# Prompt attention scores in three passes on split operands, and HGRN2 levels on running decayed keys and queries

## The chip, the cores and the metric

The kernel runs on one core of a Trainium2 chip. The metric is the device time of one execution in microseconds, taken as the median of several runs. The engines are TensorE (PE, with its weight loads shown as PEld), VectorE (DVE), ScalarE (ACT), GpSimd (POOL) and SyncE (SP), which issues most of the DMAs. Every engine works through its own queue in order and waits for others by semaphores.

## The reference

One layer of a hybrid decoder is computed for a prompt of 512 tokens and a sample group of 8 sequences of 4 tokens (544 columns together, D = 1024). The two parts that the change touches are these:

```python
# dilated attention, 8 heads of 64: three (window, dilation) patterns per query, ALiBi bias,
# the three outputs combined by their softmax denominators
s = jnp.einsum('bqhd,bqjhd->bhqj', q, kg) * (ATT_DH ** -0.5)
s = s - slopes[:, None, None] * dist
...
# HGRN2, 4 heads of 128: S_t = diag(f_t) S_{t-1} + (1 - f_t) outer i_t, o_t = S_t^T q_t, by chunks
f = lb + (1.0 - lb) * jax.nn.sigmoid(hf)
qh = jax.nn.silu(hq) * (HG_DK ** -0.5)
o, s_new = hgrn2_recurrence(qh, 1.0 - f, hi, jnp.log(f), hg_s0)
```

Around them stand the input projection (w_in), w_out, cross attention to a memory of 256 rows, and a gated feed-forward part with a short convolution (D_FF = 2816). All of it is float32.

## The kernel before, in words

All activations lie with the features on the partitions and the 544 tokens along the free axis. A dense product of float32 operands is made of three products of rounded operands (fp32r): each operand is split into a high part and a low rest, and high by high, high by low and low by high are added up in one PSUM bank. Dense banks have the tag "dense" (two of them), side work has "aux" (five) and "dec" (one). Some pairs of column blocks (`MixPair`, and `Pair` in the feed-forward part) are computed by a scheme of seven products in place of eight, whose intermediate sums are kept in SBUF.

Between the dense products PE does the side work: attention of the samples on their cache (`psd`, `psdo`, 32 columns of the array at a time), attention of the prompt (`psS` scores, `psT` transposes, `psO` values) for four pairs of heads, and HGRN2 (`psB`, `psA`, `psL`, `psin`, `psU`, `psu`, `pso`) for four heads.

`prompt_attention(p, q, k, v)` takes a pair of heads. q and k of the two heads lie on rows 0 to 63 and 64 to 127. The scores of query block qb against its 128·qb+128 keys are one float32 product per head, on 64 rows of the array. A float32 product shows as two records in the trace, one for each of its passes; an fp32r product and a transpose show as one. The blocks are grouped (0, 1), (2), (3). `softmax` adds the bias and takes the maximum on DVE and the exponent on ACT; `turn` transposes, `keep` copies to SBUF, `values` multiplies by v.

`hgrn(h, f, q, gt, v)` handles a head by levels w = 1, 2, 4, ... 64. At a level, blocks of 2w tokens have a first half (keys) and a second half (queries); `level_ops(w)` makes the decayed keys and queries `kq` on DVE and then brings the running decays G (of the keys) and f (of the queries) to the next level; `level_products` multiplies `kq` by itself in blocks of 32, 64 or 128 tokens on PE.

Nothing of the order is in the code as written: a recording layer, `Tape`, takes down all calls as steps, and `Tape.order` then runs through modelled time and sets every engine's queue. PE's main steps (the dense products) keep their order; side steps are put between them in bursts. The table `STAGES` sets, by stretch of modelled time, how much side work has to be ready before a burst begins, how long to wait for more, how far the other engines may run ahead, and how early a step has to be done before a dense product that needs it. `_Engine` holds the modelled lengths. SBUF tiles come from one pool of 60 (`A`), and a step begins only when a tile is free.

All recorded instructions carry the one line that replays them (L650), so the profile is read by the names of tiles.

Of the kernel before, what the change touches and what calls it, by code (L numbers as in the profile page):

```python
# [13 lines left out]
ALU = mybir.AluOpType  # L14
# [3 lines left out]
SEQ = 512  # L18
NB = 8
TS = 4  # L20
NS = NB * TS
# [229 lines left out]
class Tape:  # L251
# [7 lines left out]
    SLACK = 12.0  # L259
    STAGES = ((0.0, 0.99, 5.3, 12.97, 2.17), (60.0, 1.12, 3.92, 14.04, 3.2), (120.0, 1.24, 4.88, 12.15, 5.56),  # L260
              (180.0, 1.34, 4.7, 16.76, 2.71), (240.0, 0.9, 4.38, 15.81, 3.46), (300.0, 1.46, 5.82, 14.16, 5.06),
              (360.0, 0.8, 5.5, 18.48, 5.51), (425.0, 1.24, 4.59, 12.36, 5.28), (500.0, 1.39, 2.78, 18.59, 5.14),
              (740.0, 0.77, 5.29, 14.78, 3.98))
# [340 lines left out]
class _Engine:  # L604
# [5 lines left out]
    def __getattr__(self, method):  # L610
# [3 lines left out]
        def take(*args, **kw):  # L614
# [10 lines left out]
            if engine == "PE":  # L625
                n, m, k = int(np.prod(args[2].shape[1:])), outs[0].shape[0], args[1].shape[0]
                words = 4
                if method == "transpose":
                    n, length, words = 128, 0.11, 2
                elif args[1].dtype == F32R:  # L630
                    length, words = 0.0004433 * n + 0.0049, 2
                else:
                    length = 2 * max(0.112 if m == 128 and k == 128 else 0.0135,
                                     0.000842 * n * (m / 128 if m < 128 else 1.0) * (0.5 if k <= 64 else 1.0))
                lag = 0.35
            elif engine == "ACT":
# [18 lines left out]
def tile_decoder_step(ctx: ExitStack, tc: tile.TileContext, xT, memT, kwT, vw, s0, conv_in, mkT, mv, vecs, cst,  # L655
# [433 lines left out]
    class MixPair:  # L1089
# [40 lines left out]

        def keep(self, name):
            t = A(f"{name}{self.name}")
            nc.scalar.copy(t[:, :HT], self.banks["a"][:, :HT])
            return t
# [4 lines left out]
        def less(self, kept, n0):  # L1139
            nc.vector.tensor_tensor(kept[:, :HT], self.banks["c"][:, :HT], kept[:, :HT], op=ALU.subtract)  # L1140
            self.direct(1, kept, n0)

        def open(self):
            self.product("a", PD, "A11", "B11")
            self.q1 = self.keep("q")

        def middle(self):
            self.product("c", PX, "S3", "X")
            self.product("a", None, "S2", "U")
            self.z = self.keep("z")  # L1150
            sides.pump()
            self.product("d", PX, "A12", "B21")
            nc.vector.tensor_tensor(self.q1[:, :HT], self.q1[:, :HT], self.banks["d"][:, :HT], op=ALU.add)
            self.direct(0, self.q1, 0)
            self.product("a", None, "S1", "T")
            self.less(self.keep("r"), HT)
            sides.pump()
# [130 lines left out]
    def decode_finish(out):  # L1288
# [16 lines left out]
        flat = attS.rearrange("p q n -> p (q n)")  # L1305
        sq, r = A("dsq"), A("dr")
        nc.scalar.activation(sq[:, :128], flat, AF.Square)
# [11 lines left out]
    def prompt_attention(p, q, k, v):  # L1319
# [83 lines left out]
        for group in groups:  # L1403
# [11 lines left out]
            values(group)  # L1415
        att, sq, r = A(f"att{p}"), A(f"asq{p}"), A(f"ar{p}")
        nc.scalar.copy(att[:, :SEQ], po)
# [9 lines left out]
    def hgrn(h, f, q, gt, v):  # L1427
        sq_, sg_ = A(f"hqs{h}"), A(f"hgs{h}")
        with tape.together():
# [23 lines left out]
        def level_ops(w):  # L1453
# [53 lines left out]
        for w in (4, 8):  # L1507
            level_products(w, kq.pop(w))
        tmp, tmp2, sml = A(f"htm{h}"), A(f"htn{h}"), A(f"hsm{h}")
        vs, ks, ats = sml[:2 * NS, 0:128], sml[:2 * NS, 128:256], sml[:NS, 256:352]  # L1510
        nc.vector.tensor_tensor(v4(tmp), v4(bank["b"]), m4(C("mask_b")), op=ALU.mult)
        nc.vector.tensor_tensor(ats, bank["b"][:NS, 384:480], C("mask_s")[:NS, :], op=ALU.mult)
        kq[16] = level_ops(16)
# [27 lines left out]
        for i in range(2):  # L1541
# [12 lines left out]
                                C("batch")[:2 * NS, :, None].to_broadcast([2 * NS, 4, 128]), op=ALU.mult)  # L1554
        nc.vector.tensor_tensor(ats[:, :32], ats[:, :32], ats[:, 32:64], op=ALU.add)
        nc.vector.tensor_tensor(ats[:, :32], ats[:, :32], ats[:, 64:96], op=ALU.add)
        nc.vector.tensor_tensor(tmp[:, :128], tmp[:, :128], tmp[:, 128:256], op=ALU.add)
# [24 lines left out]
        inter = A(f"hin{h}", [128, 2, 128])  # L1582
        for g in range(2):
# [15 lines left out]
        pos = pin[:, 384:512]  # L1599
        nc.tensor.matmul(pos[:, :NS], vs[:NS], ats[:, :32], start=True, stop=False)  # L1600
        for i in range(2):
# [6 lines left out]
    def hgrn_norm(h, o, gt):  # L1608
        sq = A(f"hsq{h}")
        nc.scalar.activation(sq[:, :N], o[:, :N], AF.Square)  # L1610
        nc.vector.tensor_tensor(o[:, :N], o[:, :N], gt[:, :N], op=ALU.mult)
        r = A(f"hr{h}")
        rsqrt_rows(sq, 0, N, "ones", 128, r, f"hg{h}")
        nc.vector.tensor_tensor(o[:, :N], o[:, :N], r[:, :N], op=ALU.mult)
        mixed[4 + h] = split_plain(o[:, :N], f"om{h}")
# [862 lines left out]
```

## Time and profile before

| | before |
|---|---|
| median of 3 runs | 813.92 us (813.55 to 814.2) |
| span of the profiled execution | 813.0 us (instructions alone; the profiled execution's own time is not given apart from it) |
| PE busy / weight loads | 802.4 / 755.4 us |
| DVE / ACT / POOL busy | 648.5 / 445.0 / 102.8 us |
| HBM read / written | 126.17 / 8.07 MB |
| side work on attention and HGRN2 | about 76 to 306 us of the span |

A row of a timeline has start, duration, engine, operation, out<-in, shape and count. PE's products are pipelined: a row's duration includes the way through the array, and what a product costs the queue is the time from its start to the next start. A shape such as 64*128 is the part of the array used, rows by columns.

### The profile page before, as it was taken

Reading aid. Unit: us, or ns where it says so; the run is one execution under the profiler, and the core shown is the slowest. Engines: PE = TensorE matmul, PEld = TensorE weight load, DVE = VectorE, ACT = ScalarE, POOL = GpSimd, SP = SyncE. Lnnn points to the kernel's source line nnn. Section 1 sums busy time; section 2 is a strip of 40 time slices with the busy share of each in tenths; the row PEclk is TensorE's granted clock in tenths of the full one; section 3 lists DMA queues with packets and bytes.
Section 4 is the critical chain, followed back from the end, with each engine's and each line's share of the span. In section 5 each row is a group of like instructions: output and inputs, shape, how many; then the busy total and the mean of one; then the engine's idle time right before and its main releaser. Section 6 shows DMA issues by size and latency. Waiting matters only on the chain.

```text
span 813.0 us, 18994 instructions
## 1 busy us (share of the span) xinstructions
PE 802.4 (99%) x7531; PEld 755.4 (93%) x7531; DVE 648.5 (80%) x1458; ACT 445.0 (55%) x889; POOL 102.8 (13%) x186
## 2 busy tenths in 40 slices
PE   9999999999999999999999999999999999999996
PEld 9999986787889889999899999999999999999996
DVE  6996689966887897574689999997888788788854
ACT  7643365666657647454567655554554454445433
POOL 0021100010010000002201211211022012210013
PEclk9999999999999999999999999999999999999999
DMA  9449995955942454261734665655565555564503
GB/s 330 151 129 310 308 381 188 320 195 187 288 124 99 162 160 156 59 218 48 229 106 99 157 161 136 162 132 143 130 150 140 133 150 155 130 177 97 153 1 110
DMA packets 93065, 135.47 MB, mean 167 GB/s; under 512 B 6321, under 2 KB 60337, under 8 KB 92977
## 3 DMA queue, kind: packets, MB, share of 16 engines
q1 hardware_dynamic: 86208, 122.79, 46.8%
q0 software_dynamic: 5760, 10.49, 8.3%
q8 instruction: 59, 0.97, 0.5%
q10 hardware_dynamic: 1008, 0.99, 0.4%
q14 instruction: 30, 0.24, 0.1%
HBM read 126.17 MB, written 8.07 MB: 165 GB/s over the span
## 4 chain that ended last, share of the span: by engine, by line
PE 90%; DVE 5%; DMA 2%; ACT 2%; issue 1%; SPq 0%; DVEq 0%
PE ps_d L650 13%; PE ps_ag L650 7%; PE ps_au L650 7%; PE ps_wo L650 6%; PE ps_cu L650 4%; PE ps_cg L650 4%; PE ps_cq L650 3%; PE ps_dz L650 3%; PE ps_co L650 2%; PE ps_z_v L650 2%; PE ps_z_i L650 2%; PE ps_dg L650 2%; PE ps_du L650 2%; PE ps_z_Q L650 2%; PE ps_z_f L650 2%; PE ps_g L650 1%
## 5 line engine op out<-in xcount | busy, mean ns | idle before, releaser
L650 ACT CAST wh<-wr 128x1024 fp32r<-128x1024 f32 (+1 forms) x54 | 46.1, 873 | 45.3 <-PE ps_z_i L650 8.9
L650 DVE TENSOR_TENSOR wl<-wr,wh 128x1024 fp32r<-128x1024 f32 (+1 forms) x54 | 54.3, 1016 | 3.7 <-ACT wh L650 3.6
L650 DVE TENSOR_TENSOR xr<-xr,ps_d 128x256 f32<-128x256 f32 x80 | 34.6, 433 | 11.1 <-PE ps_d L650 10.2
L650 POOL COPY last<-ug 128x16 f32<-128x16 f32 (+1 forms) x44 | 22.6, 534 | 120.2 <-DVE ug L650 119.6
L650 DVE SCALAR_TENSOR_TENSOR cv<-ug,vec,cv 128x560 f32<-128x560 f32 x44 | 35.1, 798 | 2.5 <-ACT cv L650 1.9
L650 ACT ACTIVATE cv<-ug,vec 128x560 f32<-128x560 f32 x22 | 18.8, 856 | 15.5 <-DVE ug L650 15.4
L650 POOL TENSOR_TENSOR hvm<-hsm,cs 64x512 f32<-64x512 f32 x4 | 4.5, 1119 | 161.6 <-ACT hsm L650 161.6
L650 DVE TENSOR_TENSOR cv<-cv,r_ux 128x512 f32<-128x512 f32 (+1 forms) x44 | 18.7, 435 | 3.9 <-ACT cv L650 3.3
L650 ACT ACTIVATE P<-P,mx 128x128 f32<-128x128 f32 (+3 forms) x32 | 17.6, 553 | 6.7 <-DVE mx L650 6.7
L650 ACT ACTIVATE cv<-cv 128x560 f32<-128x560 f32 x22 | 14.8, 674 | 9.1 <-DVE cv L650 9.1
L624 POOL DMA_DIRECT2D S1u<-in_w_up x10 | 8.6, 863 | 87.4 <-DMA S1u<-in_w_up 27.6
L650 ACT COPY keptu<-ps_au 128x272 f32<-128x272 f32 x20 | 7.7, 386 | 21.1 <-PE ps_au L650 21.1
L650 ACT COPY keptg<-ps_ag 128x272 f32<-128x272 f32 x20 | 7.7, 385 | 21.0 <-PE ps_ag L650 20.7
L650 POOL TENSOR_SCALAR cp<-cp,cden 128x256 f32<-128x256 f32 x8 | 8.1, 1019 | 85.7 <-issue 76.2
L650 PE MATMUL ps_co<-coh,wh 128*128 128x256 f32 (+1 forms) x64 | 18.6, 291 | 0.0
L650 PE MATMUL ps_co<-coh,wl 128*128 128x256 f32 (+1 forms) x64 | 18.4, 288 | 0.0
L650 PE MATMUL ps_co<-col,wh 128*128 128x256 f32 (+1 forms) x64 | 18.4, 288 | 0.0
L650 DVE TENSOR_TENSOR xr<-xr,ps_wo 128x256 f32<-128x256 f32 (+1 forms) x16 | 6.8, 435 | 12.6 <-PE ps_wo L650 12.6
L650 DVE TENSOR_TENSOR xr<-xr,ps_dz 128x288 f32<-128x288 f32 (+1 forms) x15 | 6.6, 438 | 12.3 <-PE ps_dz L650 12.3
L650 PE MATMUL psdo<-st,dpt 128*32 128x256 f32 x224 | 16.2, 386 | 0.1
L650 ACT ACT_TABLE_LOAD x11 | 14.1, 1283 | 2.3 <-issue 2.1
L650 PE MATMUL psd<-st,qbd_win 128*32 128x224 f32 x256 | 15.4, 358 | 0.0
(3889 smaller groups left out, 3670.7 us busy)
## 6 DMA issues: line engine op xcount, KB each, us to landing
st<-in_kwT SPq DMA_DIRECT2D x32, 448.0 KB, 5.9
st<-in_vw SPq DMA_DIRECT2D x28, 512.0 KB, 5.7
wd<-in_w_down SPq DMA_DIRECT2D x32, 256.0 KB, 3.1
wr<-in_w_in SPq DMA_DIRECT2D x15, 512.0 KB, 6.6
wrg<-in_w_gate SPq DMA_DIRECT2D x10, 512.0 KB, 4.1
wru<-in_w_up SPq DMA_DIRECT2D x10, 512.0 KB, 4.5
st<-in_mkT SPq DMA_DIRECT2D x8, 512.0 KB, 6.8
wr<-in_w_out SPq DMA_DIRECT2D x8, 512.0 KB, 3.7
```

The source lines that it names most:

```text
L624: return tape.put(engine, lambda: call(*args, **kw), outs, ins, 0.1, 0.3, size)
L650: return tape.put(engine, lambda: call(*args, **kw), outs, ins, length, lag, size, port, words)
```

## The change

The scores take q and k split in high and low parts (`split_half`: a cast on ACT and a subtraction on DVE for each) and become three fp32r products a head and block, first head and second head in turn. The planner is told that an fp32r product on 64 rows takes half the time. HGRN2 no longer keeps G: a copy of k (`hkd`) and q·f (`hqd`) are themselves decayed in place, level by level; `kq` becomes a copy of their halves on ACT, and the block decays are products of the two halves' decays, small tiles in the space of `sq_`. The sample's v by token is a transpose in place of a product with the identity. `MixPair` keeps its intermediate sums in the output tiles. Several scratch tiles are reused (`PT` is `P`, `r` is `sq`, `sml` and `inter` lie in `tmp` and `tmp2`). Eight of the ten rows of `STAGES` have new numbers.

```diff
-    STAGES = ((0.0, 0.99, 5.3, 12.97, 2.17), (60.0, 1.12, 3.92, 14.04, 3.2), (120.0, 1.24, 4.88, 12.15, 5.56),
...
+    STAGES = ((0.0, 0.72, 3.13, 12.97, 2.17), (60.0, 1.31, 3.92, 16.92, 3.2), (120.0, 1.24, 3.12, 11.55, 5.56),
...
                 elif args[1].dtype == F32R:
-                    length, words = 0.0004433 * n + 0.0049, 2
+                    length, words = (0.0004433 * n + 0.0049) * (0.5 if k <= 64 else 1.0), 2
...
-        def keep(self, name):
-            t = A(f"{name}{self.name}")
-            nc.scalar.copy(t[:, :HT], self.banks["a"][:, :HT])
+        def keep(self, i, n0):
+            t = self.out[i][:, n0:n0 + HT]
+            nc.scalar.copy(t, self.banks["a"][:, :HT])
             return t
...
+        qs, ks = (split_half(t[:, :SEQ], f"{n}{p}") for n, t in (("qs", q), ("ks", k)))
...
-                for hh in range(2):
-                    rows = slice(64 * hh, 64 * hh + 64)
-                    nc.tensor.matmul(S[group, hh][:, at(qb):at(qb) + nk], q[rows, 128 * qb:128 * qb + 128],
-                                     k[rows, :nk], start=True, stop=True)
+                for i, (a, b) in enumerate(((0, 0), (0, 1), (1, 0))):
+                    for hh in range(2):
+                        rows = slice(64 * hh, 64 * hh + 64)
+                        nc.tensor.matmul(S[group, hh][:, at(qb):at(qb) + nk], qs[a][rows, 128 * qb:128 * qb + 128],
+                                         ks[b][rows, :nk], start=i == 0, stop=i == 2)
...
-                PT[group, hh] = A(f"PT{p}{group[0]}{hh}")
+                PT[group, hh] = P[group, hh]
...
-                by_token_s(v, spare)
+                nc.tensor.transpose(spare, v[:, SEQ:N], C("ident"))
...
-        G = A(f"hG{h}")
-        nc.gpsimd.memset(G[:, :N], 1.0)
...
+        kd, qd = A(f"hkd{h}"), A(f"hqd{h}")
+        nc.scalar.copy(kd[:, :N], k[:, :N])
+        nc.vector.tensor_tensor(qd[:, :N], q[:, :N], f[:, :N], op=ALU.mult)
+        decay, at = {1: f}, 0
+        for w in LEVELS:
+            count = (N if w <= 2 else SEQ) // (2 * w)
+            decay[2 * w] = sq_[:, at:at + count]
+            at += count
...
-            if w == 1:
-                nc.vector.tensor_copy(half(kq, 0), half(k, 0))
-            else:
-                nc.vector.tensor_tensor(half(kq, 0), half(k, 0), half(G, 0), op=ALU.mult)
-            nc.vector.tensor_tensor(half(kq, 1), half(q, 1), half(f, 1), op=ALU.mult)
-            last = half(f, 1)[:, :, w - 1:w].to_broadcast([128, nb, w])
-            nc.vector.tensor_tensor(half(G, 0), half(G, 0), last, op=ALU.mult)
-            last = half(f, 0)[:, :, w - 1:w].to_broadcast([128, nb, w])
-            nc.vector.tensor_tensor(half(f, 1), half(f, 1), last, op=ALU.mult)
+            whole = decay[w][:, :2 * nb].rearrange("p (b s) -> p b s", s=2)
+            nc.scalar.copy(half(kq, 0), half(kd, 0))
+            nc.scalar.copy(half(kq, 1), half(qd, 1))
+            nc.vector.tensor_tensor(half(kd, 0), half(kd, 0), whole[:, :, 1:2].to_broadcast([128, nb, w]), op=ALU.mult)
+            nc.vector.tensor_tensor(half(qd, 1), half(qd, 1), whole[:, :, 0:1].to_broadcast([128, nb, w]), op=ALU.mult)
+            nc.vector.tensor_tensor(decay[2 * w], whole[:, :, 0], whole[:, :, 1], op=ALU.mult)
...
-        ftot, ftots = small(f"ftot{h}", 4), small(f"ftots{h}", 8)
-        nc.vector.tensor_tensor(k[:, :N], k[:, :N], G[:, :N], op=ALU.mult)
-        nc.vector.tensor_copy(ftot, f[:, 127:SEQ:128])
-        nc.vector.tensor_copy(ftots, f[:, SEQ + 3:N:4])
-        nc.vector.tensor_tensor(q[:, :N], q[:, :N], f[:, :N], op=ALU.mult)
+        k, q, ftot, ftots = kd, qd, decay[128], decay[4][:, SEQ // 4:]
```

The queues that come out differ as follows.

**PE, the first score products of head pair 0.** Before, the blocks (0, 1) of the pair stand between a product of the pair g1 v0 and the next one (`ps_ag1v`, `ps_cg1v`); z_k and z_q are whole float32 tiles:

```order
L650 MATMUL ps_ag1v_392<-xm7h,S4lg1v_382 128x272
L650 MATMUL psS_420<-z_k_167,z_q_223 128x128
L650 MATMUL psS_421<-z_k_167,z_q_223 128x128
L650 MATMUL psS_420<-z_k_167,z_q_223 128x256
L650 MATMUL psS_421<-z_k_167,z_q_223 128x256
L650 MATMUL ps_cg1v_404<-mVh_239,A22hg1v_383 128x272
```

Now they stand after the first half of `ps_z_i`, with `ks0h`, `ks0l` the high and low parts of k. The end of that burst:

```order
L650 MATMUL psS_405<-ks0h,qs0l 128x256
L650 MATMUL psS_406<-ks0h,qs0l 128x256
L650 MATMUL psS_415<-ks0h,qs0h 128x384
L650 MATMUL psS_416<-ks0h,qs0h 128x384
L650 MATMUL psS_415<-ks0l,qs0h 128x384
L650 MATMUL psS_416<-ks0l,qs0h 128x384
L650 MATMUL psS_415<-ks0h,qs0l 128x384
L650 MATMUL psS_416<-ks0h,qs0l 128x384
L650 MATMUL psS_406<-cs,z_v_174 32x128
L650 MATMUL psd_394<-st_392,qbd_win 32x224 x4
L650 MATMUL ps_z_i_256_449<-xm0h,wh_444 128x288
```

The blocks (0, 1) and (2) now share one burst, and the transpose of the sample's v follows them at once; before, block (2) had a burst of its own and the product with v stood 36 rows after block (2)'s, behind `psL` and `pst_hk`.

**DVE, around the sample's v of pair 0** (`z_v_174` is the tile of v0, `hf`, `hq` are f and q of head 0). Before, the end of v0 stands behind all levels of head 0:

```order
L650 TENSOR_TENSOR hAT_195<-htm_190 32x4x32 x3
L650 COPY ftot_200<-hf_112 128x4
L650 TENSOR_TENSOR hq_113<-hq_113,hf_112 128x544
L650 TENSOR_TENSOR z_v_174<-rg1v_408,r_mix 128x272
L650 ISA P_446,mx_448<-psS_444,bias_417 128x512
```

Now it stands ahead of the levels from w = 2 on:

```order
L650 TENSOR_SCALAR mx_419<-mx_419 128x1
L650 TENSOR_TENSOR z_v_174<-z_v_174,r_mix 128x272
L650 TENSOR_TENSOR hqd_184<-hqd_184,hqs_180 128x136x2
L650 TENSOR_TENSOR hkd_183<-hkd_183,hqs_180 128x136x2
L650 TENSOR_SCALAR z_f_171<-z_f_171,lbt 128x544
```

The product that PE needs for the sample's v has moved from behind the HGRN steps of head 0 to ahead of most of them.

**PE, the long burst after `ps_z_v_256`** (sample attention `psdo`, transposes `psT`, HGRN2 blocks `psB` of head 1). A piece of it before:

```order
L650 MATMUL psdo_533<-st_525,dpt_529 32x256 x4
L650 MATMUL psdo_533<-st_588,dpt_529 32x256 x4
L650 MATMUL psT_428<-cs,P_422 128x128 x3
L650 MATMUL psT_429<-cs,P_425 128x128 x3
L650 MATMUL psdo_533<-st_589,dpt_529 32x256 x4
L650 MATMUL psB_480<-z_Q_172,hk_477 32x32 x17
L650 MATMUL psdo_533<-st_591,dpt_529 32x256 x4
L650 MATMUL psB_480<-kq_1_478 32x32 x17
L650 MATMUL psT_440<-cs,P_434 128x128 x3
```

and the same stage now:

```order
L650 MATMUL psdo_507<-st_496,dpt_503 32x256 x4
L650 MATMUL psdo_507<-st_498,dpt_503 32x256 x4
L650 MATMUL psdo_507<-st_499,dpt_503 32x256 x4
L650 MATMUL psT_413<-cs,P_407 128x128 x3
L650 MATMUL psT_414<-cs,P_410 128x128 x3
L650 MATMUL psU_206<-hvt_203,hkt_204 128x128 x4
L650 MATMUL psT_423<-cs,P_417 128x128 x3
L650 MATMUL psT_424<-cs,P_420 128x128 x3
L650 MATMUL psdo_507<-st_559,dpt_503 32x256 x4
```

More rows of one shape (32 columns, or the full array) follow each other before the shape changes. Over the whole program PE has 6461 products before and 6525 now, all 64 more of them scores; from the row sums of the cross attention's norm on, save that two side products change places, the order is the same.

More of the change, by code (lines that the diff above doesn't have):

```diff
@@ L259 @@
     SLACK = 12.0
[L260 to L262 removed]
+    STAGES = ((0.0, 0.72, 3.13, 12.97, 2.17), (60.0, 1.31, 3.92, 16.92, 3.2), (120.0, 1.24, 3.12, 11.55, 5.56),
+              (180.0, 1.34, 4.7, 11.49, 5.29), (240.0, 0.9, 4.38, 7.78, 3.46), (300.0, 1.46, 5.82, 11.44, 5.06),
+              (360.0, 0.8, 5.5, 10.31, 3.2), (425.0, 0.96, 4.59, 4.48, 5.28), (500.0, 1.39, 2.78, 18.59, 5.14),
               (740.0, 0.77, 5.29, 14.78, 3.98))
@@ L1139, in less @@
         def less(self, kept, n0):
-            nc.vector.tensor_tensor(kept[:, :HT], self.banks["c"][:, :HT], kept[:, :HT], op=ALU.subtract)
+            nc.vector.tensor_tensor(kept, self.banks["c"][:, :HT], kept, op=ALU.subtract)
             self.direct(1, kept, n0)
@@ L1144, in open @@
             self.product("a", PD, "A11", "B11")
-            self.q1 = self.keep("q")
+            self.q1 = self.keep(0, 0)
         def middle(self):
@@ L1149, in middle @@
             self.product("a", None, "S2", "U")
-            self.z = self.keep("z")
+            self.z = self.keep(1, 0)
             sides.pump()
             self.product("d", PX, "A12", "B21")
-            nc.vector.tensor_tensor(self.q1[:, :HT], self.q1[:, :HT], self.banks["d"][:, :HT], op=ALU.add)
+            nc.vector.tensor_tensor(self.q1, self.q1, self.banks["d"][:, :HT], op=ALU.add)
             self.direct(0, self.q1, 0)
             self.product("a", None, "S1", "T")
-            self.less(self.keep("r"), HT)
+            self.less(self.keep(1, HT), HT)
             sides.pump()
@@ L1305, in decode_finish @@
         flat = attS.rearrange("p q n -> p (q n)")
-        sq, r = A("dsq"), A("dr")
+        sq = r = A("dsq")
         nc.scalar.activation(sq[:, :128], flat, AF.Square)
@@ L1415, in prompt_attention @@
             values(group)
-        att, sq, r = A(f"att{p}"), A(f"asq{p}"), A(f"ar{p}")
+        att, sq = A(f"att{p}"), A(f"asq{p}")
+        r = sq
         nc.scalar.copy(att[:, :SEQ], po)
@@ L1508, in hgrn @@
             level_products(w, kq.pop(w))
-        tmp, tmp2, sml = A(f"htm{h}"), A(f"htn{h}"), A(f"hsm{h}")
-        vs, ks, ats = sml[:2 * NS, 0:128], sml[:2 * NS, 128:256], sml[:NS, 256:352]
+        tmp, tmp2 = A(f"htm{h}"), A(f"htn{h}")
+        vs, ks, ats = tmp[:2 * NS, 384:512], tmp2[:2 * NS, 384:512], tmp[:NS, 512:544]
+        own = tmp2[:NS, :96]
         nc.vector.tensor_tensor(v4(tmp), v4(bank["b"]), m4(C("mask_b")), op=ALU.mult)
-        nc.vector.tensor_tensor(ats, bank["b"][:NS, 384:480], C("mask_s")[:NS, :], op=ALU.mult)
+        nc.vector.tensor_tensor(own, bank["b"][:NS, 384:480], C("mask_s")[:NS, :], op=ALU.mult)
+        nc.vector.tensor_tensor(ats, own[:, :32], own[:, 32:64], op=ALU.add)
+        nc.vector.tensor_tensor(ats, ats, own[:, 64:96], op=ALU.add)
         kq[16] = level_ops(16)
@@ L1581, in hgrn @@
                                            op0=ALU.mult, op1=ALU.add)
-        inter = A(f"hin{h}", [128, 2, 128])
+        inter = tmp2[:, :256].rearrange("p (g v) -> p g v", g=2)
         for g in range(2):
@@ L1599, in hgrn @@
         pos = pin[:, 384:512]
-        nc.tensor.matmul(pos[:, :NS], vs[:NS], ats[:, :32], start=True, stop=False)
+        nc.tensor.matmul(pos[:, :NS], vs[:NS], ats, start=True, stop=False)
         for i in range(2):
@@ L1611, in hgrn_norm @@
         nc.vector.tensor_tensor(o[:, :N], o[:, :N], gt[:, :N], op=ALU.mult)
-        r = A(f"hr{h}")
-        rsqrt_rows(sq, 0, N, "ones", 128, r, f"hg{h}")
-        nc.vector.tensor_tensor(o[:, :N], o[:, :N], r[:, :N], op=ALU.mult)
+        rsqrt_rows(sq, 0, N, "ones", 128, sq, f"hg{h}")
+        nc.vector.tensor_tensor(o[:, :N], o[:, :N], sq[:, :N], op=ALU.mult)
         mixed[4 + h] = split_plain(o[:, :N], f"om{h}")
```

2 lines of the change are left out of this document (removed).

## The prediction

> **What bounds the kernel now.** I read the page first: the busy table, the row of the granted clock and the chain that ended last.
>
> ```profile
> span 813.0 us, 18994 instructions
> PE 802.4 (99%) x7531; PEld 755.4 (93%) x7531; DVE 648.5 (80%) x1458; ACT 445.0 (55%) x889; POOL 102.8 (13%) x186
> PEclk9999999999999999999999999999999999999999
> PE 90%; DVE 5%; DMA 2%; ACT 2%; issue 1%; SPq 0%; DVEq 0%
> ```
>
> TensorE (PE) is busy in 99% of the span, at full clock, and carries 90% of the chain. The 5% of VectorE (DVE) on the chain need not be lost time, because the chain follows one releaser at a time while PE may be at other work. So the second view is the waits of PE in the stretch that the change touches (100 to 310 us), and the third the busy time by stretch.
>
> ```profile
> PE psS L650 <- DVE z_v L650: 1.4, 1, 1.4
> ...
> 100.00:140.00 40.00, 38.53 (x592) 31.36 (x584) 36.79 (x112) 23.08 (x50) 2.11 (x3) 1.00 0.85 298
> 140.00:180.00 40.00, 39.91 (x589) 30.37 (x591) 35.52 (x110) 27.14 (x65) 2.46 (x3) 1.00 0.78 254
> 180.00:220.00 40.00, 39.90 (x461) 32.88 (x458) 27.36 (x79) 25.02 (x50) 0.00 (x0) 1.00 0.71 230
> 220.00:260.00 40.00, 40.00 (x449) 35.71 (x448) 34.38 (x96) 24.86 (x61) 2.12 (x3) 1.00 0.45 140
> 260.00:300.00 40.00, 40.00 (x542) 35.43 (x541) 33.68 (x80) 23.47 (x45) 1.92 (x2) 1.00 0.45 142
> ```
>
> PE has one visible wait there, of 1.4 us; everywhere else it goes from one product to the next. The columns are PE, weight loads, DVE, ScalarE (ACT) and GpSimd, then clock and DMA. So this kernel's time is the sum of what PE is given, and the change is worth what it takes from PE's own queue, plus that wait, less any new wait. DVE work that is saved is worth nothing by itself.
>
> **How PE's rows are priced.** The start of one row to the start of the next is what a product costs PE. This is the timeline of PE around the first two score products of head pair 0, and at the third:
>
> ```profile
> 107.25 0.96 PE L650 MATMUL psd<-st,qbd_win 128*32 128x224 f32 x16
> 108.03 0.24 PE L650 MATMUL psd<-knew,qbd_win 128*32 128x32 f32 x8
> ...
> 109.57 0.29 PE L650 MATMUL ps_ag1v<-xm7l,S4hg1v 128*128 128x272 f32 x1
> 109.69 0.29 PE L650 MATMUL ps_ag1v<-xm7h,S4lg1v 128*128 128x272 f32 x1
> 109.91 0.93 PE L650 MATMUL psS<-z_k,z_q 64*128 64x128 f32 x8
> 110.77 0.40 PE L650 MATMUL ps_cg1v<-mVh,A22hg1v 128*128 128x272 f32 x1
> 111.00 0.28 PE L650 MATMUL ps_cg1v<-mVl,A22hg1v 128*128 128x272 f32 x1
> 111.12 0.29 PE L650 MATMUL ps_cg1v<-mVh,A22lg1v 128*128 128x272 f32 x1
> ...
> 127.61 1.13 PE L650 MATMUL psS<-z_k,z_q 64*128 64x512 f32 x4
> ...
> 128.66 0.92 PEld L650 LDWEIGHTS psL<-kq 128*32 128x32 f32 x24 [0.76 <-DVE htm L650]
> ```
>
> A dense product of 272 columns costs 0.12 to 0.13 us. Where the shape of the array changes (128*128 to 64*128 at 109.69) it costs 0.22: 0.09 more. The first product after the change back (110.77) costs 0.23: 0.10 more. Into the four-column shape the entry is cheap: 16 records of psd are four passes of 224 columns and take 0.78 us. The scores of two heads (rows 0 to 63 and 64 to 127) run side by side: four records are two f32 passes by two heads, and 512 columns take 1.05 us, less 0.19 for the change of shape 0.86, or 0.84 ns a column and pass for both heads together. For psd this rate gives 4 x 224 x 0.84 ns = 0.75, so the entry was 0.03. Products on rounded operands (fp32r) of the full array are seen at 128 and 512 columns:
>
> ```profile
> 158.94 0.39 PE L650 MATMUL psr_att<-sqh_att,blk_r 128*128 128x512 f32 x1
> 159.17 0.39 PE L650 MATMUL psr_att<-sql_att,blk_r 128*128 128x512 f32 x1
> 159.41 0.60 PE L650 MATMUL pst_v<-cs,z_v 128*128 128x128 f32 x4
> 159.93 0.41 PE L650 MATMUL psS<-cs,z_v 128*32 128x128 f32 x2
> 160.27 0.39 PE L650 MATMUL ps_z_f<-xm0h,wh 128*128 128x256 f32 x1
> ...
> 305.21 0.22 PE L650 MATMUL psr_attS<-sqh_attS,blk_r 128*128 128x128 f32 x1
> 305.27 0.28 PE L650 MATMUL psr_attS<-sql_attS,blk_r 128*128 128x128 f32 x1
> ```
>
> 0.23 us for 512 columns is 0.45 ns a column, in one pass; 128 columns take 0.06.
>
> **The change, part by part.**
> *Scores.* A head pair has 128+256+384+512 = 1280 score columns. Before: two passes, 2 x 1280 x 0.84 ns = 2.15 us. After: three passes, 3 x 1280 x 0.45 ns = 1.73, if two heads still run side by side. Four pairs: **-1.7 us**. No row shows an fp32r product on 64 rows. The far end is that the heads take turns: 3.46 a pair, +5.2 for four. I take side by side, since the f32 rows of the same tiles do it.
> The Trainium skill ("TensorE: Matmul & The Clock Gate", Part 3, Measured speedup vs the span model) has 3.07x for four row tiles of 512 columns, not 4x. At that share (77%) a pair would cost an estimated 2.25 us, the term would be +0.4 and the sum -4.3; our f32 rows, 0.84 ns for two heads, show no such loss, and no run here has the fp32r case.
>
> *Sample values by token* (spare) become a transpose: one pass instead of two. The two passes take 0.34 less 0.09 for the change of shape (159.93 to 160.27); four transposes take 0.52 (159.41 to 159.93). 0.25 - 0.13, four times: **-0.5**.
>
> *Order of PE's queue.* The dense products keep their order; what stands between them is regrouped by the new table. I counted the places in the two orders where the array's shape changes: 140 before, 122 after. From dense to the four-column shape and back costs 0.09+0.03+0.09+0.10 = 0.31, so 0.155 each: 18 x 0.155 = **-2.8**. Ends: 0.12 and 0.19 each, -2.2 and -3.4.
>
> *The wait.* PE stood before psS<-cs,z_v, because DVE had z_v behind the last HGRN steps of head 0:
>
> ```profile
> 129.76 0.66 PE L650 MATMUL pst_hk<-cs,hk 128*128 128x128 f32 x4
> ...
> 130.72 0.72 DVE L650 TENSOR_TENSOR hq<-hq,hf 128x544 f32<-128x544 f32 x1
> 131.36 0.43 DVE L650 TENSOR_TENSOR z_v<-rg1v,r_mix 128x272 f32<-128x272 f32 x1
> ...
> 131.85 0.41 PE L650 MATMUL psS<-cs,z_v 128*32 128x128 f32 x2 [1.43 <-DVE z_v L650]
> 132.18 0.40 PE L650 MATMUL ps_z_v<-xm0h,wh 128*128 128x288 f32 x1
> ```
>
> In the new order both halves of that z_v stand ahead of level 2 of head 0, and hq and ftot are gone: **-1.4**. Ends: -1.4 and 0, if PE then waits for z_v at the earlier burst.
>
> *DVE, ACT, POOL.* Of DVE's four half-width products a level two go; ACT copies two halves instead.
>
> ```profile
> L650 DVE TENSOR_TENSOR kq<-hk,hG 128x256 f32<-128x256 f32 x20 | 8.3, 417 | 0.0
> L650 DVE TENSOR_TENSOR htm<-htm 128x128 f32<-128x128 f32 x4 | 1.1, 287 | 0.1
> L650 DVE TENSOR_TENSOR sql_att<-asq,sqh_att 128x512 fp32r<-128x512 f32 x4 | 2.7, 686 | 1.0 <-ACT sqh_att L650 1.0
> L650 ACT CAST sqh_att<-asq 128x512 fp32r<-128x512 f32 x4 | 2.5, 620 | 0.2
> L650 ACT ACTIVATE sq_mem<-mem 128x256 f32<-128x256 f32 x7 | 2.8, 402 | 0.0
> L650 ACT CAST wh<-wr 128x1024 fp32r<-128x1024 f32 x20 | 20.9, 1047 | 27.1 <-PE ps_z_i L650 8.5 <-PE ps_ck L650 6.0 <-PE ps_z_v L650 3.7
> ```
>
> 28 levels x 2 x 0.42 = -23.5 us on DVE; the whole-width k by G goes too (4 x 0.72, by the hq row); back come 28 small decay products (up to 272 columns, 0.29 and less at 128: about 6.5 in all) and eight subtractions for the splits, 8 x 0.69 = 5.5. Net about -14. ACT gets 56 copies x 0.40, four of full width and eight casts x 0.62: about +30. Both cost nothing on PE: in 100 to 300 us ACT is busy 123.6 of 200 and would be at 77%, DVE goes from 168 to about 154. If that cover is gone the third rival below applies. Four POOL memsets of G go; nobody waits for POOL there. The reused scratch tiles (P for PT, the output tile for kept sums) add no instruction. After the cross attention's first products PE's order is as before, so nothing is taken there.
>
> **The sum**: -1.7 - 0.5 - 2.8 - 1.4 = -6.4. The profiled span of 813.0 lies 0.9 below the median of 813.92, which the sum is taken from: **807.5 us**. A change under 0.2% (1.6 us) can't be told from none here.
>
> **Rivals.**
> *The gain is half eaten* (810.3). Scores now wait for q and k to be cast (0.62) and subtracted (0.69). If each pair's first scores wait one subtraction more, 4 x 0.7 = 2.8 comes back: 813.9 - 3.6. For it: DVE's queue is in order and 84% full in 100 to 300. Against: before, only one wait shows in all that stretch.
> *Two heads can't share the array in fp32r* (814.4, within 0.2%). An f32 pass gives a column every 0.84 ns for each of two heads, one per 0.42 ns in all; an fp32r product of the full array gives one per 0.45. If that is the rate at which PE writes results, the pair takes turns, +5.2 instead of -1.7: 813.9 - 4.7 + 5.2. The f32 rows fit this just as well; against it is only that each head has a PSUM bank of its own.
> By the Trainium skill (same page, Part 2, step 4) results leave the array "one column per cycle" through one write port, which would make this so; its packing measurement above speaks against it.
> *ACT and DVE wait for each other* (822, slower). DVE multiplies the running keys in place and must wait for ACT's copy of them; ACT's queue is in order, and a weight cast ahead of the copy takes 1.05 us; DVE's dense evacuations stand behind. If half of the 28 steps wait one cast and it reaches PE, 14 x 1.05 = 14.7: 813.9 - 6.4 + 14.7. It decides from 6.4/28 = 0.23 us a step. For it: 14 hand-overs a head that were none. Against: a head's levels are spread over tens of microseconds, ACT has 38% free, and PE works on another dense bank meanwhile.
>
> **How the numbers follow.** Forecast (805 to 809.5): 0.55. Half eaten: 0.18, also faster. Turns in the array: 0.13, nearly all within 0.2%. Hand-overs: 0.14, slower. So faster 0.73, same 0.12, slower 0.15. The low end is -3.4 for the shapes and 1.3 for small waits that PE's rows hide as pitch, with the other terms as they are: 813.9 - 8.3, rounded down to 805. The high end takes in turns: 814.8. Outside are the hand-overs and a little on either side. The forecast's own range is 805 to 809.5.
>
> **What would show it.** Scores: a pass of 512 columns for two heads every 0.23 us (0.46 if in turns), bursts of 64*128 rows with three passes. Shapes: 18 fewer, PE's busy time down by about as much as the span. The wait: no PE row before psS<-cs,z_v of pair 0. DVE down by some 14 us, ACT up by 30, with neither moving the span. Wrong would be: new waits of PE on qs, ks, kq or a z tile that add up to over 3 us, or DVE idle behind ACT's kq copies.

## The result: 809.5 us for 814.06, and the profile after

Five executions of the changed kernel took 809.19 to 809.89 us (median 809.5), five of the kernel before 813.55 to 815.54 (median 814.06) on the same chip. The ratio is 0.9933, with a 95% interval of 0.9922 to 0.9945: 4.5 to 6.3 us less. The forecast of 807.5 was 2 us too low; the range (805 to 814.8) holds the result, at the upper edge of the forecast's own range (805 to 809.5). Two of the twelve executions of e10 below (1301 and 2746 us, against 813 to 815 for the others) were slow and are left out of its median and its ratio.

The page of the profile after, in the same lines as before:

```profile
span 808.1 us, 19075 instructions
PE 797.6 (99%) x7559; PEld 756.8 (94%) x7559; DVE 639.3 (79%) x1426; ACT 468.3 (58%) x957; POOL 96.9 (12%) x182
PE 92%; ACT 3%; DVE 3%; DMA 1%; issue 0%; ACTq 0%; DVEq 0%
```

The span is 4.9 us shorter and PE's busy time 4.8 us: the gain was taken from PE's own queue. DVE lost 9.2 us and ACT gained 23.3, and neither shows in the span. Two of the rows of PE's waits (engine, tile <- releaser: us in all, times, longest):

```profile
PE psin L650 <- ACT htn L650: 0.8, 1, 0.8
PE ps_first L650 <- ACT wfh L650: 0.5, 1, 0.5
```

The wait of 1.43 us for z_v is gone. One of 0.83 us has come at 277.69, where the products of head 3's queries with the sample states stand behind ScalarE's copy `htn`. The 0.5 us on `wfh` lies in the first 10 us, which the change does not touch; it differs from run to run. With it and 0.2 more at `ps_z_q`, all of PE's waits together are 3.1 us after and 3.0 before, so no net gain comes from waits.

The timeline of PE at the scores of head pair 0, blocks (0, 1) first and block (3) below:

```profile
115.29 0.28 PE L650 MATMUL ps_z_i<-xm7h,wl 128*128 128x256 f32 x1
115.50 0.33 PE L650 MATMUL psS<-ks0h,qs0h 64*128 64x128 f32 x2
115.67 0.28 PE L650 MATMUL psS<-ks0l,qs0h 64*128 64x128 f32 x2
115.78 0.27 PE L650 MATMUL psS<-ks0h,qs0l 64*128 64x128 f32 x2
115.89 0.33 PE L650 MATMUL psS<-ks0h,qs0h 64*128 64x256 f32 x2
116.06 0.28 PE L650 MATMUL psS<-ks0l,qs0h 64*128 64x256 f32 x2
...
128.47 0.50 PE L650 MATMUL psS<-ks0h,qs0h 64*128 64x512 f32 x2
128.80 0.39 PE L650 MATMUL psS<-ks0l,qs0h 64*128 64x512 f32 x2
129.03 0.39 PE L650 MATMUL psS<-ks0h,qs0l 64*128 64x512 f32 x2
129.35 0.46 PE L650 MATMUL psA<-kq 128*32 128x32 f32 x32
129.63 0.41 PE L650 MATMUL psA<-cs,z_i 128*32 128x128 f32 x4
130.12 0.64 PE L650 MATMUL psdo<-st,dpt 128*32 128x256 f32 x8
```

Each row is one pass for both heads (x2). A pass of 512 columns takes 0.23 us (128.80 to 129.03), as forecast for two heads side by side. But a pass of 128 columns takes 0.11 (115.67 to 115.78), not 0.06, and the first pass of 256 columns 0.17, not 0.115.

### The profile page after: what moved, and what is told of

Read it like the earlier page. It is cut to its first block, busy times and chain, and to the rows that moved or that the text cites. A ratio compares the mean times of both kernels' runs of the same rounds, so it can differ in the third digit from the quotient of the medians.

```text
span 808.1 us, 19075 instructions
## 1 busy us (share of the span) xinstructions
PE 797.6 (99%) x7559; PEld 756.8 (94%) x7559; DVE 639.3 (79%) x1426; ACT 468.3 (58%) x957; POOL 96.9 (12%) x182
## 4 chain that ended last, share of the span: by engine, by line
PE 92%; ACT 3%; DVE 3%; DMA 1%; issue 0%; ACTq 0%; DVEq 0%
PE ps_d L650 13%; PE ps_au L650 7%; PE ps_ag L650 7%; PE ps_wo L650 6%; PE ps_cu L650 4%; PE ps_cg L650 4%; PE ps_co L650 3%; PE ps_dz L650 3%; PE ps_cq L650 3%; PE ps_z_i L650 2%; PE ps_z_v L650 2%; PE ps_dg L650 2%; PE ps_du L650 2%; PE psd L650 2%; PE psdo L650 2%; PE ps_z_Q L650 2%
## 5 line engine op out<-in xcount | busy, mean ns | idle before, releaser
L650 POOL COPY last<-ug 128x16 f32<-128x16 f32 (+1 forms) x44 | 20.2, 484 | 109.1 <-DVE ug L650 108.4
L650 POOL TENSOR_TENSOR hvm<-htm,cs 64x512 f32<-64x512 f32 x4 | 4.3, 1064 | 172.7 <-ACT htm L650 172.7
L650 DVE CUSTOM_DVE_ANT_0 P<-psS,bias 128x128 f32<-128x128 f32 (+3 forms) x32 | 13.9, 486 | 1.8 <-PE psS L650 1.7
```

The costliest lines, as they stand in the source:

```text
L650: return tape.put(engine, lambda: call(*args, **kw), outs, ins, length, lag, size, port, words)
```

## The experiments

All times are medians; "before" ran on the same chip, and the ratio (95% interval) is the number to compare. 0.001 of the ratio is 0.8 us. The number of changes of the array's shape is counted in the order of PE's rows.

| kernel | shape changes | us | before, us | ratio |
|---|---|---|---|---|
| the change | 122 | 809.5 | 814.06 | 0.9933 (0.9922 to 0.9945) |
| e1 f32 scores, same order | 122 | 809.89 | 814.75 | 0.9937 (0.9925 to 0.9949) |
| e2 changed kernel, old table | 133 | 820.8 | 814.75 | 1.0068 (1.0054 to 1.0083) |
| e3 before, split scores only | 132 | 817.91 | 814.75 | 1.0043 (1.0031 to 1.0055) |
| e4 changed kernel, grouped by shape | 97 | 806.02 | 814.75 | 0.9891 (0.9876 to 0.9905) |
| e5 40 dense extras | 122 | 815.08 | 815.3 | 0.9995 (0.9983 to 1.0008) |
| e6 40 extras, 32 columns | 202 | 814.08 | 815.3 | 0.9985 (0.9973 to 0.9996) |
| e7 40 extras, 64 columns | 202 | 814.01 | 815.3 | 0.9991 (0.9979 to 1.0002) |
| e8 heads in turn | 122 | 810.85 | 815.3 | 0.9942 (0.992 to 0.9964) |
| e10 before, grouped by shape | 114 | 813.93 | 815.03 | 0.999 (0.998 to 1.0001) |
| e11 before, new table only | 139 | 814.44 | 815.03 | 0.9988 (0.9978 to 0.9999) |
| e12 ScalarE's copies twice | 122 | 828.95 | 815.63 | 1.0166 (1.0147 to 1.0184) |

Theory A is the prediction's: the change is worth what it takes from PE's own queue. The first four kernels set it against two others.

**e1: what are the split scores worth?** The recorded order is the changed kernel's, row for row; only the score products differ.

```
-  for i, (a, b) in enumerate(((0, 0), (0, 1), (1, 0))):
-      for hh in range(2): ... qs[a][rows, ...], ks[b][rows, :nk], start=i == 0, stop=i == 2
+  for hh in range(2): ... q[rows, ...], k[rows, :nk], start=True, stop=True
```

> The changed kernel with its scores taken from q and k in f32 again (two passes); the splits are still computed but not read, and all other products stand in the changed kernel's order, so 122 changes of the array's shape. Theory A (the change is worth what it takes from PE's own queue: scores, shape changes, one wait): the trace gives 2.18 us a head pair in f32 and 1.91 split, so 4 x 0.27 = +1.1, 810.6 us. Theory B (the 4.5 us come mostly from the split scores, and the regrouped order is worth nothing): 813 to 814.

Measured: 0.4 us above the change (ratios 0.9937 and 0.9933, not told apart). In the traces the score rows take 10.61 us for 9.56, 1.05 more, as theory A had it. In the time only 0.4 shows, and that can't be told from nothing. The timeline of PE at block (3) in e1 shows one place where the split scores lose what they gained:

```profile
128.77 1.13 PE L653 MATMUL psS<-z_k,z_q 64*128 64x512 f32 x4
129.82 0.46 PE L653 MATMUL psA<-kq 128*32 128x32 f32 x32
130.10 0.41 PE L653 MATMUL psA<-cs,z_i 128*32 128x128 f32 x4
130.34 0.64 PE L653 MATMUL psdo<-st,dpt 128*32 128x256 f32 x8
```

Here the products with z_i take 0.24 us and `psdo` follows at once; in the changed kernel the same row takes 0.49 (129.63 to 130.12). There PE came earlier and `psdo` did not start earlier, without a wait on record. Theory B falls, since the time without the split scores is 3 us below its 813. By the rows they take 1.05 us from PE's queue; how much of that reaches the time is open, between nothing and about 1.

**e2: the changed kernel under the old table**

```
-  STAGES = ((0.0, 0.72, 3.13, 12.97, 2.17), (60.0, 1.31, 3.92, 16.92, 3.2), ...
+  STAGES = ((0.0, 0.99, 5.3, 12.97, 2.17), (60.0, 1.12, 3.92, 14.04, 3.2), ...
```

> The changed kernel with the old table of stages: same work, another order, 133 changes of shape for 122. Theory A: priced one by one (0.09 to leave, 0.015 to 0.105 to enter) 20.45 us of changes for 18.74, +1.7, 811.2 us, plus at most 1.5 if PE waits for the sample's v again. Theory B: 809.5, no change beyond new waits.

Measured: 820.8, 11 us over the change. Theory A had 1.7 (and 1.5 for a wait) and misses by 8; theory B misses too. It is the prediction's third rival, ScalarE and DVE handing over. PE's wait, and the rows of PE, DVE and ACT that lead to it:

```profile
PE psA L650 <- ACT kq L650: 4.6, 1, 4.6
```

```profile
124.91 0.56 DVE L650 TENSOR_TENSOR htm<-psB,cs 128x384 f32<-128x384 f32 x1 [5.05 <-PE psA L650]
125.98 0.41 DVE L650 TENSOR_TENSOR hqd<-hqd,hqs 128x256 f32<-128x256 f32 x1
```

```profile
128.95 1.03 ACT L650 CAST wh<-wr 128x1024 fp32r<-128x1024 f32 x1
129.88 0.40 ACT L650 COPY kq<-hqd 128x256 f32<-128x256 f32 x1
130.19 0.40 ACT L650 COPY kq<-hkd 128x256 f32<-128x256 f32 x1
```

```profile
130.64 0.66 PE L650 MATMUL psA<-kq 128*32 128x32 f32 x32 [4.62 <-ACT kq L650]
131.09 0.62 PE L650 MATMUL psA<-cs,z_i 128*32 128x128 f32 x4
131.64 0.58 PE L650 MATMUL ps_z_v<-xm0h,wh 128*128 128x256 f32 x1
132.02 0.42 PE L650 MATMUL ps_z_v<-xm0l,wh 128*128 128x256 f32 x1
132.24 0.41 PE L650 MATMUL ps_z_v<-xm0h,wl 128*128 128x256 f32 x1
```

DVE stood 5.05 us for PE's diagonal products, with the next level's products queued behind. When it had made them, ACT still had the softmax and a weight cast of 1.03 us ahead of the two copies. PE, whose queue had come to that level, stood 4.62 us. Then its dense rows take 0.22 us instead of 0.12 for some 4 us. The windows (us, PE, weight loads, DVE, ACT, POOL, granted clock) say why:

```profile
132.00:136.00 4.00, 4.00 (x20) 4.00 (x20) 3.87 (x10) 2.04 (x6) 1.86 (x1) 0.50 0.47 137
136.00:140.00 4.00, 4.00 (x34) 3.84 (x36) 1.31 (x7) 0.14 (x1) 0.00 (x0) 0.98 0.00 0
```

The granted clock is 0.50 there, and the rows of `ps_z_v` cost 2.0 us more in all than before the change, where the wait of 1.43 us left the clock at 1.00.

**e3: the kernel before, with only the scores split.** The same product lines as in e1, the other way round, put into the kernel before, with its old table.

> The kernel before, its table kept, with only the scores split into three passes. They bring the planner to 132 changes of shape for 140 by themselves (20.03 us for 21.52). Theory A: -1.1 for the scores, -1.5 for the changes: 811.4 us, 1.4 less if the wait for the sample's v goes too. Theory B: all or most of the gain, 809.5 to 810.

Measured: 817.91, slower than before by 2.5 to 4.5 us; both theories miss. PE stands 4.7 us in all between 70 and 310 us. The longest wait, and the window behind it:

```profile
142.22 0.66 PE L650 MATMUL pst_v<-cs,z_v 128*128 128x128 f32 x4 [2.07 <-ACT vnew L650]
```

```profile
144.00:146.00 2.00, 2.00 (x12) 2.00 (x11) 1.97 (x8) 2.00 (x6) 0.00 (x0) 0.50 1.02 328
```

Transposes of v stand for ACT's copy `vnew`, and the clock halves again, after 2.07 us of idleness: the rows of `ps_z_f` cost 1.5 us more. The Trainium skill ("TensorE: Matmul & The Clock Gate", Part 1, What's actually happening) has the clock halved after an idle window of about 3.4 us. Here 2.07 us were enough (with transposes and column products behind it), and 1.43 before the change were not. But the length of the wait doesn't decide it alone: in the profiles of e8 and e5 the clock drops behind a wait of 0.9 us at `htn` (its mean from 280 to 284 us is 0.58 and 0.59), while the change itself, with 0.83 us of waiting at the same place, has 1.00 there; and in e11 it is 0.50 from 296 to 300 us with no wait of PE on record in that stretch. What sets it off is open. As in e2, the table was not set for this work.

**e4: the same work and table, other order.** When a burst of side products is open, the planner took the one with the earliest due time; now one of another shape than PE's counts 2 us later.

```
-  s = min(side, key=lambda s: (s.begin, s.number))
+  s = min(side, key=lambda s: (s.begin + 2.0 * (s.forms[0] != form), s.number))
+  form = s.forms[-1]
```

> The changed kernel, same work and table; where several side products are ready, the planner takes those of the shape that PE has, unless another is due 2 us earlier: 97 changes of shape for 122 (15.13 us for 18.74). Theory A: -3.6, 805.9 us, less what new waits take. Theory B: 809.5. Rival C (a regrouped order delays what others wait for): above 809.5, with new waits of PE in 76 to 306 us.

Measured: 806.02, against 805.9 for theory A. The ratios differ by 0.0042, 3.4 us for 25 changes of shape, 0.14 each (the intervals leave 1.4 to 5.6 us). Of the 25, 10 lie beside a dense product and 15 between side products; this is the only experiment that prices the second kind. The profiled execution was the slowest of the four (808.38 us); in it the dense rows at the edges of the bursts cost 0.95 us less than in the change and the side rows 2.0 less. PE's waits from 70 to 310 us are 0.7 us in all, as many as in the change (0.8). This kernel is the fastest here, with no arithmetic altered.

**e5, e6, e7: is it the shape?** Ahead of 40 dense products of the gate and up projections stands one short product (32 columns streamed), with 128, 32 or 64 columns of the weights.

```
+  if first:
+      nc.tensor.matmul(ps[:c, :32], w[0][0][:, :c], xs[0][0][:, :32], start=True, stop=True)
```

> The changed kernel with one short product more (32 columns on the full array) ahead of each of 40 dense products of the gate and up projections; its result is overwritten by the product behind it. No change of shape is added, the rest stands in the same order. It is the control of the next two. 128 columns cost 0.06 us in such a row, so 40 x 0.06 = +2.4: 811.9 us; up to 40 x 0.11 = +4.4 if the load of the weights sets it.

> The same 40 short products with 32 of the weights' columns (32 rows of output), so that each leaves the full array's shape and comes back: 80 changes of shape more, the order the same. Theory A: 40 x 0.31 = 12.2, so about 821.5 to 822, 10 us over the control. Rival B (changes of shape are not what the regrouped order saved): within 2 us of the control.

> The same with 64 columns of the weights: 80 changes to and from the two-column shape. Theory A by the trace's rows (0.09 to leave, 0.05 to enter, 0.09 and 0.105 back): 40 x 0.34 = 13.6, about 823 us. Rival B: within 2 us of the control.

Measured: 4 to 5 us over the change for all three. The control came out as its upper case; e6 and e7 went against theory A, which had 10 us more. PE's rows in e6, the extra and the first dense product in one row:

```profile
452.02 0.28 PE L650 MATMUL ps_u<-ux7h,wl 128*128 128x256 f32 x1
452.14 0.40 PE L650 MATMUL ps_ag<-ux0h,whg 128*32 128x32 f32 x2
452.38 0.29 PE L650 MATMUL ps_ag<-ux0l,whg 128*128 128x272 f32 x1
```

The dense row ahead costs its usual 0.12, and the two rows together 0.24: 0.125 and 0.11 for the extra, in all three kernels. (The x2 row holds the extra and the dense product behind it.) So a row marked 128*32 need not cost a change of shape. That made theory A doubtful as it stood, and the next run asked which rows do.

**e8: do the heads share the array, or only stand side by side in the queue?**

```
-  for i, (a, b) in enumerate(((0, 0), (0, 1), (1, 0))):
-      for hh in range(2):
+  for hh in range(2):
+      for i, (a, b) in enumerate(((0, 0), (0, 1), (1, 0))):
```

> The changed kernel with the three passes of one head ahead of those of the other, in the same places of the queue, so that only one of the six passes of a block still stands beside one of the other head. If two heads share the array: 4 pairs x 1280 columns x 2 more passes x 0.45 ns = +4.6, 814.1 us. If the array writes one column at a time whatever the heads do: 809.5.

Measured: 810.85; the ratio's interval (0.992 to 0.9964) holds the change's 0.9933. The expectation of +4.6 fell, but not because the heads can't share. PE's timeline of block (3), where the queue now has all three passes of head 0 and then those of head 1:

```profile
128.15 0.51 PE L650 MATMUL psS<-ks0h,qs0h 64*128 64x512 f32 x2
128.49 0.40 PE L650 MATMUL psS<-ks0l,qs0h 64*128 64x512 f32 x2
128.72 0.40 PE L650 MATMUL psS<-ks0h,qs0l 64*128 64x512 f32 x2
```

The first row is the first pass of both heads: head 1's, fourth in the queue, starts 0.01 us after head 0's and 0.33 before the second in the queue. PE ran the two halves of the array apart. The score rows take 9.61 us in all, 9.56 in the change.

**e9: which rows pay.** One extra product of 256 columns ahead of each of the 40 dense products, of eight kinds in turn: full array, 128*32 and 64*128, each on rounded and on f32 operands; 128*64 on f32; and, as one kind, four f32 products on the four 32-column parts. Rounded 128*64 is not among them; e7 has it.

> The changed kernel with one extra product of 256 columns ahead of each of 40 dense products, of eight kinds in turn (five places each): full array, 128*32, 128*64 and 64*128, on rounded (fp32r) and on f32 operands; its result is overwritten. Read by the start of one row to the next: what the dense row ahead costs over its usual 0.12 to 0.13, and what the dense row behind costs over it. Theory A (every change of shape costs): 0.09 ahead and 0.10 behind for every kind but the two of the full array. Theory D (after the run with 40 short products of 32 columns, where it did not cost: the weights of a part of the array can be loaded during the product before only for rounded column tiles): 0.09 and 0.10 for f32 on 128*32 and 128*64 and for 64*128 of either type, nothing for rounded 128*32 and for the full array.

Measured, in one profiled execution (831.89 us). PE's rows around an extra on 32 columns of rounded weights, one on 32 columns of f32 weights (two passes), and one on 64 rows of rounded weights. The second row of each fence holds the extra and the first dense product behind it:

```profile
463.90 0.29 PE L650 MATMUL ps_ag<-Th,S1g2l 128*128 128x272 f32 x1
464.02 0.41 PE L650 MATMUL ps_au<-ux0h,whu 128*32 128x256 f32 x2
464.26 0.29 PE L650 MATMUL ps_au<-ux0l,whu 128*128 128x272 f32 x1
```

```profile
471.53 0.29 PE L650 MATMUL ps_d<-h1h,wd_0l 128*128 128x288 f32 x1
471.75 0.94 PE L650 MATMUL ps_cu<-Xh,S3u2h 128*32 128x256 f32 x3
472.52 0.29 PE L650 MATMUL ps_cu<-Xl,S3u2h 128*128 128x272 f32 x1
```

```profile
493.33 0.29 PE L650 MATMUL ps_d<-h1h,wd_3l 128*128 128x288 f32 x1
493.56 0.70 PE L650 MATMUL ps_au<-ux0h,whu 64*128 64x256 f32 x2
494.09 0.29 PE L650 MATMUL ps_au<-ux0l,whu 128*128 128x272 f32 x1
```

In the first, every row keeps its pitch (0.12, then 0.24 for two). In the second and third the dense row ahead costs 0.22 instead of 0.13, 0.09 more. The second extra with the dense product behind takes 0.77: two passes of 0.215, 0.125 for the dense product, and 0.21 more. The third takes 0.53 for 0.24. The five places of each kind agree to about 0.01. Over the kinds: 0.09 ahead and 0.10 behind for f32 on 128*32 and 128*64 and for 64*128 of either type, and none of it for rounded 128*32 or the rounded full array, as theory D said. With what the extra's own row loses, a change there and back costs 0.32 us for f32 on 128*32, 0.34 for f32 on 128*64 and 0.39 for 64*128; the prediction had 0.31 for the first. An f32 extra on the full array costs nothing either:

```profile
460.56 0.72 PE L650 MATMUL ps_cg<-Xh,S3g2h 128*128 128x256 f32 x3
461.12 0.29 PE L650 MATMUL ps_cg<-Xl,S3g2h 128*128 128x272 f32 x1
```

Its two passes and the dense product behind take 0.56 us to the next start: twice 0.215 and 0.125. In the trace the loads say the same: ahead of `psd` the load starts only when the dense product has streamed (127.89 in the change, 0.21 after the dense row's start), ahead of a rounded 128*32 product it starts with the dense row (452.02 in e6). The side products of this kernel on parts of the array are all f32 or 64-row, so the count of 140 and 122 stands, and beside dense products (53 of the 140, 46 of the 122) the price too; between side products it rests on e4. e6 and e7 had used the kind that is free.

**e10 and e11: the old work, grouped; and the old work under the new table**

> The kernel before, its work and its table kept, with the rule that groups ready side products by shape: 114 changes for 140 (17.58 us for 21.52). Theory A: -3.9, about 810 us. Rival C (any other order brings new waits of PE, as the old table did with the new work): 814 or more, with waits of PE in 76 to 306 us.

> The kernel before with only the new table: 139 changes for 140. Theory A: 814 us, up to 1.5 less if the wait for the sample's v goes. Rival B (the table alone carries the gain): 809.5 to 811. Rival C (a table serves only the work that it was made for): above 815, with new waits of PE.

Measured: -0.1% each, inside or at the edge of noise. e11 lies by theory A, which had up to 1.5 us for the wait: no wait of PE is left from 70 to 310 us, and the ratio gives 1.0 us less (0.1 to 1.8). With 139 changes left, the table alone brings no more than that. In e10, 26 changes fewer should be -3.9, and the old wait of 1.4 is gone as well, but three new waits of PE stand in the trace, which is rival C:

```profile
PE psL L657 <- ACT hAT L657: 1.4, 1, 1.4
PE psin L657 <- DVE hq L657: 1.2, 1, 1.2
PE psr_hg L657 <- DVE mx L657: 0.9, 1, 0.9
```

With 3.7 us of waits in all from 70 to 310 us the sum is -1.6; the medians show -1.1, the ratio -0.8, the profiled span (810.7 for 813.0) -2.3.

**e12: how much room does ScalarE have?** Each copy of running keys and queries is issued twice; the planner does not know it.

> The changed kernel with each of ScalarE's 56 copies of running keys and queries made twice, the order of all engines unchanged: 56 x 0.42 = 23.5 us more on ScalarE, which goes from 152 to about 175 of the 200 us from 100 to 300. If the copies lie beside other work (the prediction's cover): under 1 us more, 809.5 to 810.5. If DVE's and ScalarE's hand-overs are on the path (the prediction's third rival): about 0.42 us a level for the levels that PE waits for; with half of 28, +5.9 and more, 815 us or above, with waits of PE on kq.

Measured: 828.95, 19 us over the change (ratios 1.0166 and 0.9933). 23.5 us of work on an engine that is busy 58% of the span cost 19. The two largest rows of PE's waits, and the window behind the longest:

```profile
PE psin L651 <- ACT htn L651: 3.4, 1, 3.4
PE psA L651 <- ACT kq L651: 2.7, 2, 1.9
```

```profile
292.00:296.00 4.00, 3.81 (x60) 1.88 (x64) 2.37 (x8) 1.66 (x5) 0.00 (x0) 0.50 0.37 131
```

PE waits 11.3 us in all from 70 to 310 us. The clock is at 0.50 three times, for some 3.4 us from 127.7 and from 158.4 and for 10.2 from 291.5, at the longest wait: 17 us, which at half the clock is an estimated 8.5 us of lost work at most. The two together are about the 19 us.

## Why the prediction was right, point by point

*Scores, -1.7.* Right in mechanism, too large. Two heads share the array in fp32r (0.23 us per 512 columns), so the second rival is out. But a pass costs no less than 0.11 us, while I took 0.45 ns a column down to 128. The 0.06 that I read for 128 columns (305.21 to 305.27) was one step, into a product whose weights had been loaded beside the row ahead; the next step there is 0.11 as well (305.27 to 305.38). By the rows a pair takes 1.91 us against 2.18 in f32: -1.1, and e1 can't tell how much of that arrives. The weight load of each pass is the likely floor: the loads of the 128-column passes start 0.11 apart (115.61, 115.72, 115.83), those of the two heads side by side; no run varied that.

*Sample values, -0.5.* The rows of the spare product go from eight to four, and from 1.34 us to 0.49 with their changes of shape. No run took it alone.

*Shape changes, -2.8.* The step that carries the result, and right. The records count 140 and 122. The price, read from four rows before, is confirmed by e9 beside dense products (0.09 and 0.10) and in time by e4 (0.14 each for 25). What the other terms leave of the change's 4.9 us is 3.4: 4.9 less 1.0 (score rows), 0.5 (spare) and 0.6 (waits), plus 0.6 for the first 10 us and a wait on z_q. That is at the far end of -2.2 to -3.4, and has the small hidden gaps in it. The two traces show it more directly: from start to start, without the waits on record, the products whose number and shape the change leaves alone take 2.8 us less in the new order (0.7 in dense rows, 2.1 in side rows); the score rows take 1.3 less and the spare product 0.85, their own changes of shape included. That is the whole 4.9. What the step lacked is the condition: it is f32 column parts and row parts that pay, not every change of the shape in the records.

*The wait, -1.4.* It is gone, but 0.8 came at another place, on ACT's `htn`. I had bounded this by PE waiting for z_v earlier; the new wait is on another chain. Net -0.6. This and the scores are the two terms that make up most of the 2 us between 807.5 and 809.5: they fell short by 0.8 and 0.7, and the shapes gave back 0.6, so that the result's place inside the forecast's range is in part luck.

*DVE and ACT, nothing.* DVE fell by 9.2 us (14 forecast), ACT rose by 23.3 (30 forecast), and in the new order it is hidden. The reason I gave, ACT's 38% of free time and PE at another bank meanwhile, is not enough, as e12 and e2 show. What hides the hand-overs is, by these two runs, an order in which PE comes to a level after its copies are due, made by a planner that knows their lengths under a table set for this work; no run shows it apart. With the old table 11 us are lost, and with the copies made longer than the planner knows 19 are. The rival I gave 0.14 is a real mechanism; its threshold of 0.23 us a step was right in kind (e12 adds 0.84 a level and loses 0.67, a part of it by the clock).

*Half eaten.* PE waits for no split. What came back (0.8 at `htn`, about 0.4 in the first 10 us of the profiled run) is not that rival's.

## What to carry to other kernels

Where PE is busy 99% of the time, count what its queue pays between the products: here 122 changes of the array's shape cost some 19 us (at the 0.155 of the prediction), and one line in the planner that takes ready products of one shape together gained 3.4 us without altering the work (with the old work the same line, in e10, gained 0.8 by the ratio, barely told from nothing, as new waits took the rest). An engine that is idle 40% of the time may still have no room: judge added work by when its result is asked for, and set the order anew for it, since old work under a new table, new work under the old one, and half of the change alone gained little or lost. And measure a suspected cost with the very kind of instruction that pays it.

## What the runs showed of the hardware that I had not expected

- Products on rounded operands that use 32 or 64 columns of the weights, starting at column 0, follow a dense product and are followed by one at no cost (e9: 0.00 of 0.09 and 0.10 for 32 columns; e6 and e7: as much as on the full array, for 32 and 64), though the records give them another shape; f32 ones of the same shape pay both (e9).
- The start of a PE record need not be the time when the array is free for it: in e9 the dense product behind an f32 product on the full array starts 0.03 us after that one's second pass and takes 0.315 to the next start, in five places, yet the three cost 0.56, no more than twice 0.215 and 0.125. A single long row is no cost; add up to the next product that keeps its step.
- Products on the two row halves of the array do not start in the order of the queue: in e8 the fourth product started 0.33 us before the second. The Trainium skill ("TensorE: Matmul & The Clock Gate", Part 3, The mechanism) has products start and end strictly in order; here the measurement decides. It holds for two halves of 64 rows and four products' distance, which is all these runs show.
- A short product of 32 columns costs 0.11 us (e5, e6 and e7 alike), not the 0.014 that 32 columns at 0.45 ns would take. The loads of the full weights behind it start 0.11 apart (452.14 and 452.25 in e6), so the load, with no longer product to hide behind, is the likely reason.
